# Which of the sums of weights in two gate pairs is made by a transfer and which by VectorE, and the order in which their chunks are loaded

## The chip, the cores and the metric

The kernel runs on one core of one Trainium2 chip. The metric is the device time of one execution in microseconds (us); the time of a kernel is the median of several runs. Beside it stands one execution taken with the hardware profiler, which gives the time of every instruction and transfer.

## The reference

One decoder block on 512 tokens of width 1024, in float32. Its largest part is a projection of the normalised input by one wide weight matrix; two branches use slices of it, and sigmoid gates merge them:

```python
hn = rmsnorm(x, g_mix)
proj = einsum('bsd,de->bse', hn, w_in)          # 1024 x 14344
(xa, ba, ca, za, q, k, v, o, zb, ig, fg, ga, gb) = split(proj)
ya = (ba * causal_short_conv(ca * xa) * silu(za)) @ w_a_out
hb = mlstm_chunkwise(q, k, v, ig + .., fg + ..)  # 4 heads
yb = (sigmoid(o) * rmsnorm(hb) * silu(zb)) @ w_b_out
merged = sigmoid(ga) * ya + sigmoid(gb) * yb
x = x + merged @ w_o
x = x + sigmoid(rmsnorm(x) @ w_ple_gate) * (p @ w_ple)
out = rmsnorm(x)
```

The change concerns the slices for `gb` and `ga`, each 1024 columns wide: the two gate pairs of this document.

## The kernel before

**Split numbers.** Each product in float32 is made of three matmuls of a shorter type (`mm3`, L215). Every operand is therefore cut into a high part, a copy made by ScalarE (ACT, `whi`, L164), and a low part, the rest, made by VectorE (DVE, `wlo`, L165).

**Chunks and operands.** Weights come from HBM in chunks of 512 rows by 512 columns (1 MB, 128 partitions of four row blocks), into four slots of a pool `wraw` (NRAW, L33). The list `chunks` holds the chunks in the order in which they are loaded; the list `operands` holds what TensorE (PE) uses one after the other, each entry with the sums that are to be made after it has been split.

**Pairs.** Two column ranges p1 and p2 form a pair (`pair`, L84). Its weights are a 2 x 2 block matrix: b11 and b21 are the upper and lower 512 rows of p1, b12 and b22 those of p2. `strassen` (L305) multiplies such a pair in seven products (0 to 6) in place of eight, which needs sums of weights. In the kernel before, for a gate pair: product 0 uses b11; then b11 += b12; product 1 uses b21; product 2 uses b11, then b11 += b22; product 3 uses b22, and b12 += b22 is made; product 4 uses b11, then b11 += b21; product 5 uses b12; product 6 uses b11. A sum is made either by DVE (L169, both chunks lie in slots) or by a transfer that reads the chunk from HBM and adds it to what the slot holds, issued from GpSimd's queue (POOL, L171). `on_dve` says which: 0 all by transfers, 1 the third sum (b12 += b22) by DVE, 2 the others too. With 2, which only the two gate pairs have (L108), DVE made b11 += b12, b11 += b22 and b12 += b22, and a transfer made b11 += b21.

**The order of the work.** All engines but the load queue (SP) follow the order in which the program is written. `strassen` issues the matmuls of half a product (one PSUM bank), then calls `step` and through it `tick` (L200): first work on the results of the half before, then one half of the split of the next operand (`split_half`, L162), then the generators in `active`. So operand j + 1 is split while product j runs, one half (256 of its 512 rows) in each tick, and the sums that are listed with an operand follow the split of the same half. The split tiles exist twice (`wsplit`, two buffers).

**Loads.** When the second half of operand i has been split, `done(i)` (L175) gives back the chunks whose last use it was (`last_use`, L129) and `load_free` (L148) loads the next chunks of the list into the free slots, on SP (L144). A chunk that DVE reads as an addend is in use until that sum; one that a transfer adds is read from HBM and needs no slot for it. In the gate pairs before, slots came free after the splits for products 1, 3, 5 and 6.

**Beside the gate pairs.** A gate pair (GB in head 0's turn, GA in head 2's) follows the pair of the ZB columns of two heads, whose last results are still worked on while product 0 and 1 of the gate pair run (`sink_z`, L964: two multiplications by DVE per tile, L968 or L972 and L973, and stores of `z_d` on POOL's queue, L969). In the gate pair itself run: the transposes of the finished head (`turn`, L788, L799), the sigmoid of the gate and its store on ACT's queue (`sink_gate`, L767, L770, L771), and the reload and split of the next head's q and k (`recut`, L808: transfers on SP, L814, after 7 ticks; split by ACT and DVE in four further ticks, L224 and L225). Behind the gate pair comes the pair V and O of the next head, with all sums by transfers.

Of the kernel before, what the change touches and what calls it, by code (L numbers as in the profile page):

```python
# [29 lines left out]
HC = 4  # L30
# [6 lines left out]
def hybrid_block(ctx, tc, x, p, g_mix, w_in, conv_w, conv_b, w_a_out, b_gates, g_head,  # L37
# [31 lines left out]
    chunks, operands = [], []  # L69
    H2 = S // 2  # L70

    def chunk(view, k0, pieces):
        got, pos = [], 0
        for c, n in pieces:
            got.append((view[:, k0:k0 + HC, c:c + n], slice(0, HC), slice(pos, pos + n)))
            pos += n
        chunks.append(got)
        return len(chunks) - 1
# [5 lines left out]
    def pair(view, p1, p2, on_dve=0):  # L84

        where = ((p1, 0), (p2, 0), (p1, HC), (p2, HC)) if on_dve == 2 else ((p1, 0), (p1, HC), (p2, 0), (p2, HC))
        b11, b21, b12, b22 = (chunk(view, k, p) for p, k in where)
        if on_dve == 2:  # L90
            b12, b21 = b21, b12
        e2, e3 = (dve if on_dve >= n else None for n in (2, 1))
        t3 = [(b12, b22, e3)]
        operands.extend([(b11, [(b11, b12, e2)]), (b21, [] if e3 else t3), (b11, [(b11, b22, e2)]),
                         (b22, t3 if e3 else []), (b11, [(b11, b21, None)]), (b12, []), (b11, [])])


    chunks.append([(w_ple_v[:, k:k + 1, n * CW:(n + 1) * CW], slice(2 * n + k, 2 * n + k + 1), slice(0, CW))
# [5 lines left out]
    for h in range(NH):  # L104
        pair(w_in_v, [(V + h * DV, DV)], [(O + h * DV, DV)])
        if h % 2 == 0:
            pair(w_in_v, [(ZB + h * DV, DV)], [(ZB + (h + 1) * DV, DV)])
            pair(w_in_v, [((GB, GA)[h // 2], CW)], [((GB, GA)[h // 2] + CW, CW)], 2)  # L108
        elif h == 1:
            pair(w_in_v, *([(Q + i * DK, DK), (K + i * DK, DK)] for i in (2, 3)), 1)  # L110
    for c in range(0, KT * P, 2 * P):
        pair(w_in_v, *([(o + c, 2 * P) for o in os] for os in ((XA, CA), (BA, ZA))), 1)
    for n in range(2):
        block(w_a_v, [(n * CW, CW)])

    b11, b21, b22, b12 = ([chunk(w_b_v, (2 * g + r) * HC, [(n * CW, CW)]) for g in range(2)]
                          for r, n in ((0, 0), (1, 0), (1, 1), (0, 1)))
# [1208 lines left out]
```

## Time and profile before

| | us |
|---|---|
| median of 3 runs | 864.0 (863.95 to 864.03) |
| the profiled execution: its own time | 863.96 |
| the profiled execution: span from its first to its last instruction | 862.2 |
| mean granted clock of TensorE in it | 0.997 |
| first gate pair and what adjoins it | about 155 to 210 |
| second gate pair and what adjoins it | about 379 to 434 |

Moved bytes: 167.58 MB in 100,138 packets, of them 70.86 MB on POOL's queue (q0) and 90.97 MB on SP's (q1).

How to read the rows below. A row of a timeline has the start in us, the duration in us, the engine, the line, the operation, the output and inputs by the program's names with their shape, and the count; in brackets stands how long the engine was idle before it and what released it. A row of a stretch has from and to, its length, then for each engine its busy time and its number of instructions, and at the end TensorE's granted clock, the busy share of the DMA engines and GB/s. A row of the chain of waits has start, duration and what it was. PE is TensorE (matmuls), PEld its weight loads, DVE VectorE, ACT ScalarE, POOL GpSimd, SPq the load queue. Idle time on an engine that isn't the bottleneck costs nothing.

### The profile page before, as it was taken

The page shows a single profiled execution, that of the slowest core. Times are in us where ns is not written, and L with a number is a line of the kernel's source. Part 1 is how long each engine was busy: PE and PEld are TensorE (multiplying, and loading weights), DVE is VectorE, ACT ScalarE, POOL GpSimd, SP SyncE. Part 2 cuts the span into 40 slices and gives each one's busy share as a digit, 9 for nine tenths or more (in the row PEclk, how much of TensorE's full clock was granted, in tenths as well). Part 3 has the DMA queues.
Part 4 walks back from the last instruction along what each step waited for, and adds up shares of the span by engine and source line. Part 5 has one row for each costly group of instructions (what it writes and reads, how often), then busy time and mean ns, then how long its engine had stood idle before and what let it go on. Part 6 is the DMA issues. An engine that isn't in the chain of part 4 may idle for free.

```text
span 862.2 us, 12152 instructions
## 1 busy us (share of the span) xinstructions
PE 849.0 (98%) x4658; PEld 735.8 (85%) x4658; DVE 630.4 (73%) x813; ACT 483.9 (56%) x702; POOL 218.0 (25%) x221
## 2 busy tenths in 40 slices
PE   9999999999999999999999999999999999999996
PEld 7888888787889988878788999999998888888885
DVE  5786667966767576778568679897986778964465
ACT  7467655657755566565675555545453256634343
POOL 5103222113224322211214323333410212130031
PEclk9999999999999999999999999999999999999998
DMA  9749669589968998775999599899997487884002
GB/s 311 265 135 187 156 133 222 184 235 254 256 135 199 240 224 181 182 183 201 260 243 226 109 243 152 205 175 187 182 346 285 100 196 192 224 319 151 1 1 97
DMA packets 100138, 167.58 MB, mean 194 GB/s; under 512 B 5420, under 2 KB 45920, under 8 KB 98800
## 3 DMA queue, kind: packets, MB, share of 16 engines
q0 software_dynamic: 38672, 70.86, 42.3%
q1 hardware_dynamic: 58544, 90.97, 32.2%
q10 hardware_dynamic: 2864, 4.98, 1.6%
q8 instruction: 36, 0.59, 0.3%
q14 instruction: 22, 0.18, 0.1%
HBM read 150.01 MB, written 16.78 MB: 193 GB/s over the span
## 4 chain that ended last, share of the span: by engine, by line
PE 83%; issue 6%; DVE 4%; DMA 4%; ACT 3%; ACTq 0%; POOL 0%; SPq 0%; POOLq 0%; DVEq 0%
PE mm L218 25%; PE mm L217 25%; PE mm L219 25%; DMA wraw<-in_w_in 2%; DVE wlo L165 1%; PE pv L217 1%; PE pv L218 1%; PE pv L219 1%; ACT whi L164 1%; DMA xin<-in_x 1%; DMA z_d<-c 1%; PE sc L219 1%; PE sc L218 1%; PE sc L217 1%; DVE wraw L169 1%
## 5 line engine op out<-in xcount | busy, mean ns | idle before, releaser
L165 DVE TENSOR_TENSOR wlo<-wraw,whi 128x1024 fp32r<-128x1024 f32 x238 | 298.2, 1256 | 123.0 <-ACT whi L164 121.9
L164 ACT ACTIVATE whi<-wraw 128x1024 fp32r<-128x1024 f32 x240 | 250.8, 1054 | 105.2 <-PE mm L219 45.3
L171 POOL DMA_DIRECT2D wraw<-in_w_in x112 | 136.7, 1416 | 310.0 <-DVE wlo L165 227.1
L333 ACT ACTIVATE s<-mm 128x512 f32<-128x512 f32 x84 | 50.2, 598 | 99.9 <-PE mm L219 97.8
L217 PE MATMUL mm<-whi,hs 128*128 128x512 f32 x256 | 99.9, 390 | 0.0
L218 PE MATMUL mm<-wlo,hs 128*128 128x512 f32 x256 | 99.8, 390 | 0.0
L219 PE MATMUL mm<-whi,hs 128*128 128x512 f32 x256 | 99.7, 389 | 0.0
L217 PE MATMUL mm<-hn_hi,whi 128*128 128x256 f32 (+1 forms) x304 | 93.4, 307 | 0.0
L219 PE MATMUL mm<-hn_hi,wlo 128*128 128x256 f32 (+1 forms) x304 | 93.0, 306 | 0.0
L218 PE MATMUL mm<-hn_lo,whi 128*128 128x256 f32 (+1 forms) x304 | 92.9, 306 | 0.0
L217 PE MATMUL mm<-hs,whi 128*128 128x256 f32 x320 | 90.9, 284 | 0.0
L218 PE MATMUL mm<-hs,whi 128*128 128x256 f32 x320 | 90.5, 283 | 0.0
L219 PE MATMUL mm<-hs,wlo 128*128 128x256 f32 x320 | 90.5, 283 | 0.0
L218 PE MATMUL mm<-wlo,hn_hi 128*128 128x512 f32 x192 | 75.9, 396 | 3.1 <-DVE wlo L165 2.8
L217 PE MATMUL mm<-whi,hn_hi 128*128 128x512 f32 x192 | 75.6, 394 | 0.0
L219 PE MATMUL mm<-whi,hn_lo 128*128 128x512 f32 x192 | 74.9, 390 | 0.0
L218 PEld LDWEIGHTS mm<-hs,whi 128*128 128x128 f32 x320 | 61.4, 192 | 0.0
L217 PEld LDWEIGHTS mm<-hs,whi 128*128 128x128 f32 x320 | 61.4, 192 | 0.0
L219 PEld LDWEIGHTS mm<-hs,wlo 128*128 128x128 f32 x320 | 61.4, 192 | 0.0
L219 PEld LDWEIGHTS mm<-hn_hi,wlo 128*128 128x128 f32 x304 | 58.1, 191 | 2.8 <-POOL wlo L165 0.3
L218 PEld LDWEIGHTS mm<-hn_lo,whi 128*128 128x128 f32 x304 | 58.1, 191 | 2.4
L217 PEld LDWEIGHTS mm<-hn_hi,whi 128*128 128x128 f32 x304 | 58.1, 191 | 2.3
(306 smaller groups left out, 1673.9 us busy)
## 6 DMA issues: line engine op xcount, KB each, us to landing
wraw<-in_w_in SPq DMA_DIRECT2D x32, 1024.0 KB, 5.6
wraw<-in_w_in POOLq DMA_DIRECT2D x52, 512.0 KB, 7.9
wraw<-in_w_in SPq DMA_DIRECT2D x48, 512.0 KB, 5.3
wraw<-in_w_in POOLq DMA_DIRECT2D x60, 256.0 KB, 5.8
wraw<-in_w_b_out SPq DMA_DIRECT2D x7, 1024.0 KB, 6.2
wraw<-in_w_b_out POOLq DMA_DIRECT2D x12, 512.0 KB, 6.6
yt_d<-yc POOLq DMA_DIRECT2D x4, 1024.0 KB, 4.9
wraw<-in_w_a_out SPq DMA_DIRECT2D x4, 1024.0 KB, 6.1
```

The source lines that it names most:

```text
L164: act.activation(hi, t, AF.Copy)
L165: (e_lo or dve).tensor_tensor(lo, t, hi.bitcast(F32), ALU.subtract)
L169: eng.tensor_tensor(raws[to][:, ks, :], raws[to][:, ks, :], raws[c][:, ks, :], ALU.add)
L171: nc.gpsimd.dma_start(raws[to][:, ks, cs], src[:, ks, :], accum_op=ALU.add)
L217: pe.matmul(ps, lhsT=a[0], rhs=b[0], start=first, stop=False, **kw)
L218: pe.matmul(ps, lhsT=a[0], rhs=b[1], start=False, stop=False, **kw)
L219: pe.matmul(ps, lhsT=a[1], rhs=b[0], start=False, stop=last, **kw)
L333: act.activation(to[i], src, AF.Copy, scale=scale)
```

## The change

For `on_dve` 2 the chunks are listed in the order b11, b21, b22, b12 (before: b11, b12, b21, b22). The sum after product 0's operand, b11 += b12, becomes an adding transfer; the sum after product 4's, b11 += b21, becomes an addition by DVE. The second and third sum stay with DVE. Since b21 is now an addend of DVE, its slot is in use until the split for product 4; slots come free after the splits for products 3, 4, 5 and 6. b12 has to lie in its slot by the third sum, at product 3.

```diff
-        where = ((p1, 0), (p2, 0), (p1, HC), (p2, HC)) if on_dve == 2 else ((p1, 0), (p1, HC), (p2, 0), (p2, HC))
+        where = ((p1, 0), (p1, HC), (p2, HC), (p2, 0)) if on_dve == 2 else ((p1, 0), (p1, HC), (p2, 0), (p2, HC))
         b11, b21, b12, b22 = (chunk(view, k, p) for p, k in where)
         if on_dve == 2:
-            b12, b21 = b21, b12
+            b12, b22 = b22, b12
         e2, e3 = (dve if on_dve >= n else None for n in (2, 1))
         t3 = [(b12, b22, e3)]
-        operands.extend([(b11, [(b11, b12, e2)]), (b21, [] if e3 else t3), (b11, [(b11, b22, e2)]),
-                         (b22, t3 if e3 else []), (b11, [(b11, b21, None)]), (b12, []), (b11, [])])
+        operands.extend([(b11, [(b11, b12, None)]), (b21, [] if e3 else t3), (b11, [(b11, b22, e2)]),
+                         (b22, t3 if e3 else []), (b11, [(b11, b21, e2)]), (b12, []), (b11, [])])
```

For the other values of `on_dve` the order and the sums are the same as before.

## The prediction

> **What bounds the kernel now.** I read the page first, then the busy time of three equal stretches: one without a gate pair, and one round each of the two gate pairs that the change touches.
>
> ```profile
> span 862.2 us, 12152 instructions
> PE 849.0 (98%) x4658; PEld 735.8 (85%) x4658; DVE 630.4 (73%) x813; ACT 483.9 (56%) x702; POOL 218.0 (25%) x221
> ...
> 100.00:155.00 55.00, 55.00 (x248) 45.70 (x247) 37.86 (x52) 33.50 (x49) 11.93 (x12) 1.00 0.78 182
> 155.00:210.00 55.00, 53.44 (x238) 42.61 (x237) 41.26 (x44) 35.23 (x49) 9.42 (x10) 1.00 0.76 222
> 379.00:434.00 55.00, 53.46 (x238) 42.56 (x237) 40.73 (x44) 35.27 (x49) 9.35 (x10) 1.00 0.77 223
> 160.00:168.00 8.00, 7.52 (x31) 5.33 (x30) 7.93 (x10) 5.58 (x7) 0.54 (x1) 1.00 0.17 66
> ```
>
> PE is the bound, at full granted clock (1.00), so time can only come from its pauses. Between 100 and 155 us it has none; in both gate stretches it has, and by nearly the same amount (53.44 and 53.46 of 55). The busy column understates the pauses, since a matmul is drawn about 0.4 us long while they start 0.23 us apart; so I read the starts in the first gate pair.
>
> ```profile
> 155.01 0.39 PE L217 MATMUL mm<-whi,hn_hi 128*128 128x512 f32 x1
> ...
> 160.22 0.39 PE L219 MATMUL mm<-whi,hn_lo 128*128 128x512 f32 x1
> 160.45 0.39 PE L217 MATMUL mm<-whi,hn_hi 128*128 128x512 f32 x1
> 161.18 0.50 PE L218 MATMUL mm<-wlo,hn_hi 128*128 128x512 f32 x1 [0.34 <-DVE wlo L165]
> 161.52 0.40 PE L219 MATMUL mm<-whi,hn_lo 128*128 128x512 f32 x1
> ...
> 166.76 0.40 PE L217 MATMUL mm<-whi,hn_hi 128*128 128x512 f32 x1
> 167.29 0.50 PE L218 MATMUL mm<-wlo,hn_hi 128*128 128x512 f32 x1
> ...
> 172.23 1.03 PE L799 MATMUL pty<-ident,gty 128*128 128x128 f32 x8
> 173.02 0.48 PE L217 MATMUL mm<-whi,hs 128*128 128x512 f32 x1
> ...
> 196.39 0.39 PE L217 MATMUL mm<-whi,hn_hi 128*128 128x512 f32 x1
> 197.10 0.50 PE L218 MATMUL mm<-wlo,hn_hi 128*128 128x512 f32 x1 [0.33 <-DVE wlo L165]
> ...
> 202.45 0.39 PE L217 MATMUL mm<-whi,hn_hi 128*128 128x512 f32 x1
> 203.60 0.50 PE L218 MATMUL mm<-wlo,hn_hi 128*128 128x512 f32 x1 [0.76 <-DVE wlo L165]
> ```
>
> Every pause is at a matmul that wants the low half of a weight split (wlo). A regular start follows the last by 0.227 us (23 steps from 155.01 to 160.22, and 160.22 to 160.45 again). Against that, the first pause costs 161.18 - 160.45 - 0.23 = 0.50, and 0.11 more as the pipe refills (161.52 follows by 0.34): 0.61 us. With the same 0.11, the others cost 0.41, 0.59 and 1.03. The four make 2.64 us. By place they are: product 0 (A) and product 1 (B) of the gate pair, product 6 (C), and product 0 of the V/O pair behind it (D). Products of a pair are counted 0 to 6 here, and each weight block is split in two halves.
>
> What released these low halves is shown by the chain of waits in the same stretch:
>
> ```profile
> 155.58 1.23 DVE wlo L165
> 156.83 1.23 DVE wraw L169
> ...
> 159.90 1.23 DVE wlo L165
> 161.16 1.23 DVE wraw L169
> ...
> 181.86 9.80 DMA wraw<-in_w_in
> ...
> 197.73 1.05 ACT whi L164
> ...
> 201.23 1.07 ACT whi L164
> 202.32 1.24 DVE wlo L165
> 203.60 0.50 PE mm L218
> ```
>
> A and B come from DVE, which has no gap there (7.93 of 8.00 us busy from 160 to 168) and has to do the two halves of "b11 += b12" (L169, 156.83 and 161.16) between the splits. C and D come from a transfer: "b11 += b21", issued at 181.86, lands 9.80 us later, and only then can ACT split the sum for product 6:
>
> ```profile
> 163.15 1.05 ACT L164 ACTIVATE whi<-wraw 128x1024 fp32r<-128x1024 f32 x1
> ...
> 165.90 2.00 ACT L164 ACTIVATE whi<-wraw 128x1024 fp32r<-128x1024 f32 x2
> ...
> 191.74 1.06 ACT L164 ACTIVATE whi<-wraw 128x1024 fp32r<-128x1024 f32 x1 [1.51 <-DMA wraw<-in_w_in]
> 192.71 0.61 ACT L224 ACTIVATE qk<-qk_raw 128x512 fp32r<-128x512 f32 x1
> ```
>
> ACT loses 1.51 us at 191.74 and, being full with q/k cuts, sigmoids and its own DMA issues, doesn't make it up before the split at 201.23.
>
> **The change part by part.** Nothing is removed in all: per gate pair two DVE adds of 1.23 us and two 512 KB adding transfers change places, and the chunks are loaded in the order b11, b21, b22, b12.
>
> *The DVE adds leave product 0.* The second low half of product 0 stands behind one of them: from 159.90 it moves to 158.7, and its matmul could start at 161.18 - 1.23 = 159.95, before PE asks for it (160.45 + 0.23 = 160.68). A goes. B's low half stands behind both adds; ACT has its high half at 163.15 + 1.05 = 164.2, so the low half ends at about 165.5, while PE arrives at 166.76 + 0.23 - 0.61 = 166.4. B goes: 0.61 + 0.41 = 1.02 us.
>
> *The DVE adds arrive in product 4's split.* There DVE waits for ACT and PE:
>
> ```profile
> 180.33 2.36 DVE L165 TENSOR_TENSOR wlo<-wraw,whi 128x1024 fp32r<-128x1024 f32 x2 [0.36 <-ACT whi L164]
> 183.93 1.23 DVE L165 TENSOR_TENSOR wlo<-wraw,whi 128x1024 fp32r<-128x1024 f32 x1 [1.23 <-ACT whi L164]
> 187.55 0.69 DVE L337 TENSOR_TENSOR c<-s,mm 128x512 f32<-128x512 f32 x1 [2.39 <-ACT s L333]
> ```
>
> The idle time is 0.36 + 1.23 + 2.39 = 3.98 us, the adds take 2.46: hidden. Product 5's first split would slide from 183.93 to about 185.2, four us before that product starts. Without this cover they would cost what A and B cost now.
>
> *The adding transfer leaves product 4.* The sum is then ready in SBUF by about 185, so ACT's 1.51 us go, and every step of ACT's run behind it is that much earlier. C (0.59) goes. For D the low half's matmul could start at 203.60 - 1.51 = 202.09; PE, itself earlier by C, arrives at 202.45 + 0.23 - 0.59 = 202.09. That is an exact tie, so I leave 0.2 of D's 1.03: 0.59 + 0.83 = 1.42 us.
>
> *The adding transfer arrives in product 0.* POOL issues one half after the low half at 155.58 (so at 156.8), the other after that at 158.7 (so at 159.9). Both must land before ACT splits product 2, now 165.90 and about 166.9, then 0.6 earlier. That leaves 8.5 and 6.4 us. How long such a transfer takes, and what else goes on:
>
> ```profile
> DMA to landing us min/median/max: 4.4/6.2/13.7
> ...
> z_d<-c POOLq DMA_DIRECT2D x3, 256.0 KB, 3.4
> ```
>
> The first row is for all adding transfers of the program (L171). The second is the three POOL stores between 155 and 168, in the middle of DVE's full stretch. In 160 to 168 the DMA engines are busy 0.17, so I take the median or less: no wait. A late landing is also cushioned. Product 2 starts at 173.02 and wants its second low half 7 matmuls on, at 174.6, less the 1.0 gained: 173.6. From ACT's split to that matmul takes 203.60 - 201.23 = 2.37, so the sum may land at 171.2, 11.3 us after its issue. On POOL the new issues precede the z_d stores of the pair before, which wait for later DVE work anyway; nothing queued there is held.
>
> *The loads.* A slot now comes free at products 3, 4, 5, 6 instead of 1, 3, 5, 6 (b21 is kept for the late add). The next pair's first chunk takes the place that its second has now, on SP:
>
> ```profile
> 179.25 0.34 SPq L814 DMA_DIRECT2D qk_raw<-qk_d  x1
> 180.05 0.37 SPq L144 DMA_DIRECT2D wraw<-in_w_in  x1
> ...
> DMA to landing us min/median/max: 3.3/7.8/10.5
> ```
>
> It is wanted at 197.73, less the gain: 16 us after 180, enough. The second chunk waits for the moved add (about 185) and is wanted a product later than the first. Within the gate pair each chunk is loaded at least as early, relative to its first use, as now. The q/k reloads (L814; their time to landing is the last row) stay where they are if SP keeps its order. No cost.
>
> *Sum.* Per pair 1.02 + 1.42 = 2.44. The count of matmuls allows a check: 238 instructions in 55 us, 16 of them short transposes (eight take 0.79 us, from 172.23 to 173.02), 222 x 0.227 + 1.6 = 52.0, so about 3.0 are lost where I can name 2.64. Of the other 0.4 (small hesitations at product starts, some of them at the transposes, which stay) I take 0.3. The two gate pairs are alike (53.44 and 53.46), so 2 x 2.74 = 5.5 us. The profiled execution took 863.96 (its span of 862.2 and 1.8 round it, which the change doesn't touch), the median is 864.0: **858.5 us**.
>
> **The rivals.** *Half the gain.* If SP's new order puts the second chunk's load ahead of the q/k reloads, these are issued after the moved add, at about 185 instead of 179 on, and land 7.8 later, at about 193, where ACT wants them at 192.71 - 1.51 = 191.2, and earlier still by the 1.0 gained. One DMA wait of ACT replaces the other, and C and D stay: 863.96 - 2 x 1.02 = 861.9, or 861 with part of the small ones. For it: in program order the freed slot's load does come just before the reloads. Against: SP's present order has the first reload ahead of a load that was due two steps before it. Chance 0.11.
>
> *No change.* The pauses at A and B go, but PE then only reaches a later limit sooner: ACT's run from 191.74 to 201.23 has no slack, so if it is bound by something else than the 1.51, C and D grow by what A and B gave back. 864 within 0.2%. Against: ACT was idle for 1.51 us right before that run, so it starts it without arrears. This case also covers the case that the order of the queues leaves the adds where they cost the same. Chance 0.08.
>
> *Slower: the moved transfer lands late.* Place: ACT's split for product 2. Each us past 11.3 costs 2 (two pairs); past 14.0 the gain is used up, past 14.9 the kernel is slower by over 0.2%. The largest landing of any adding transfer is 13.7. [...] Against: the three z_d stores in the same full stretch, issued by the same queue, landed in 3.4 us. [...] Chance 0.05.
>
> **How the numbers follow.** The forecast has the remaining 0.76. Its own range is 857.4 (all of the 3.0 and a little more per pair) to 860.0 (D and the small ones stay). To hold 8 in 10 the range reaches to the half gain: 857.3 to 862.0. A change under 0.2% (1.7 us) can't be told from none here, so faster means below 862.3: the forecast and nearly all of the half gain, 0.86; same 0.08; slower 0.06, the late landing and a little for what isn't thought of.
>
> **What would show it.** Right: matmul starts at A, B and C 0.23 us apart; PE about 54.5 or more of 55 busy in both gate stretches; DVE adds at about 181 and 184, none at 156 to 162; two POOL transfers at about 157 and 160 landing in under 7 us; ACT's split for product 6 without a DMA wait. Wrong: ACT waiting for a DMA at product 2's split or at the q/k cuts, PE pauses of new origin at products 2 or 3, or the pauses C and D as long as now.

## The result and the profile after

The changed kernel takes 858.0 us (857.67 to 858.62, 6 runs), the kernel before 864.31 us in the same comparison (863.95 to 865.08, 6 runs). The ratio is 0.9926, with a 95% interval of 0.9914 to 0.9939: about 6.3 us less, where the prediction had said 858.5 us. The profiled execution spans 856.3 us (before 862.2).

The stretches that hold the gate pairs, and the eight us in which DVE had been full, in the kernel after (columns as before; 376 to 431 is the second gate pair, which now starts 3 us earlier):

```profile
155.00:210.00 55.00, 55.00 (x250) 45.05 (x249) 42.58 (x45) 35.55 (x50) 10.82 (x11) 1.00 0.82 231
...
376.00:431.00 55.00, 55.00 (x250) 45.06 (x249) 42.57 (x45) 35.59 (x50) 10.85 (x11) 1.00 0.83 232
160.00:168.00 8.00, 8.00 (x39) 6.66 (x38) 7.08 (x10) 4.14 (x6) 1.78 (x2) 1.00 0.92 191
```

PE no longer pauses visibly (55.00 of 55, before 53.44 and 53.46) and gets 250 instructions into the stretch where 238 fitted. DVE has gaps from 160 to 168 (7.08 of 8, before 7.93). The DMA engines, which had been busy 0.17 there, are busy 0.92: POOL's queue alone, with the moved transfer and the `z_d` stores. At the places of A and B the matmuls follow without a pause, as these steps of the kernel after show:

```profile
160.66 0.39 PE L217 MATMUL mm<-whi,hn_hi 128*128 128x512 f32 x1
160.88 0.39 PE L218 MATMUL mm<-wlo,hn_hi 128*128 128x512 f32 x1
...
166.10 0.39 PE L217 MATMUL mm<-whi,hn_hi 128*128 128x512 f32 x1
166.32 0.39 PE L218 MATMUL mm<-wlo,hn_hi 128*128 128x512 f32 x1
```

DVE, POOL, ACT and SP in the first gate pair after, for the steps that the prediction named:

```profile
158.84 1.22 DVE L165 TENSOR_TENSOR wlo<-wraw,whi 128x1024 fp32r<-128x1024 f32 x1
...
180.46 1.23 DVE L169 TENSOR_TENSOR wraw<-wraw,wraw 128x1024 f32<-128x1024 f32 x1
...
182.85 1.23 DVE L169 TENSOR_TENSOR wraw<-wraw,wraw 128x1024 f32<-128x1024 f32 x1
```
```profile
157.30 1.23 POOL L171 DMA_DIRECT2D wraw<-in_w_in  x1 [1.62 <-DVE wlo L165]
...
160.36 1.19 POOL L171 DMA_DIRECT2D wraw<-in_w_in  x1 [1.24 <-DVE wlo L165]
```
```profile
165.43 1.05 ACT L164 ACTIVATE whi<-wraw 128x1024 fp32r<-128x1024 f32 x1
168.10 1.06 ACT L164 ACTIVATE whi<-wraw 128x1024 fp32r<-128x1024 f32 x1 [1.61 <-DMA wraw<-in_w_in]
...
188.50 0.60 ACT L333 ACTIVATE s<-mm 128x512 f32<-128x512 f32 x1 [1.17 <-PE mm L219]
188.99 1.05 ACT L164 ACTIVATE whi<-wraw 128x1024 fp32r<-128x1024 f32 x1
```
```profile
178.20 0.34 SPq L814 DMA_DIRECT2D qk_raw<-qk_d  x1
178.91 0.37 SPq L144 DMA_DIRECT2D wraw<-in_w_in  x1
```

The low half that waited at 159.90 is made at 158.84, the adds run at 180.46 and 182.85, and the split for product 6 (188.99) follows the PSUM copy without a DMA wait. SP kept its order. One thing is new: ACT now waits 1.61 us for a transfer at the split for product 2 (168.10).

A ruler for the rest of this text is the matmul that opens the scores of a head (`pnb`, L835): its four starts in the trace cut the program into the two gate stretches, the stretch between them and the tail. The columns are in us; all rows come from one profiled execution each, and the last column is the median of all executions.

| kernel | 1st gate stretch | between | 2nd gate stretch | last `pnb` to last matmul | median, us |
|---|---|---|---|---|---|
| before | 131.51 | 92.41 | 131.57 | 419.33 | 864.31 |
| after | 128.52 | 92.41 | 128.51 | 419.33 | 858.0 |
| both by transfer | 131.45 | 92.48 | 130.01 | 419.31 | 862.1 |
| both by DVE | 129.97 | 93.10 | 129.89 | 419.31 | 860.9 |
| new sums, old order | 128.52 | 93.01 | 128.51 | 419.31 | 858.47 |
| old sums, new order | 135.56 | 92.63 | 134.88 | 419.34 | 871.81 |
| first transfer late | 132.38 | 92.45 | 130.91 | 420.05 | 865.18 |
| first transfer a plain copy | 128.52 | 92.41 | 128.53 | 419.30 | 858.04 |
| before, gate stores on POOL | 131.30 | 94.16 | 131.42 | 419.57 | 865.49 |
| after, gate stores on POOL | 128.32 | 92.43 | 128.30 | 420.79 | 858.96 |
| before, gate stores on SP | 129.94 | 93.86 | 130.13 | 420.05 | 863.15 |
| after, gate stores on SP | 128.31 | 92.41 | 128.30 | 419.34 | 857.59 |

All of the gain lies in the two gate stretches, 2.99 and 3.06 us; the stretch between and the tail have the same length to 0.01 us, and what precedes the first `pnb` is 0.2 us longer in the trace of the kernel after (79.12 beside 78.91).

A gate stretch can be cut once more, at the first transposes of the finished head (L799, at 168.58 in the kernel before): A and B lie ahead of them, C and D behind.

| kernel | 1st and 2nd gate stretch, up to the transposes (A, B) | from the transposes on (C, D) |
|---|---|---|
| before | 89.67 and 89.63 | 41.84 and 41.94 |
| after | 88.34 and 88.35 | 40.18 and 40.16 |
| both by transfer | 88.34 and 88.35 | 43.11 and 41.66 |
| both by DVE | 89.76 and 89.69 | 40.21 and 40.20 |
| before, gate stores on SP | 89.70 and 89.63 | 40.24 and 40.50 |

So A and B with the small pauses near them were worth 1.3 us in each stretch, C and D 1.7 to 1.8.

### The profile page after: what moved, and what is told of

It reads as the page before. It is cut to its first block, busy times and chain, and to the rows that moved or that the text cites. A ratio compares the mean times of both kernels' runs of the same rounds, so it can differ in the third digit from the quotient of the medians.

```text
span 856.3 us, 12144 instructions
## 1 busy us (share of the span) xinstructions
PE 845.6 (99%) x4658; PEld 735.4 (86%) x4658; DVE 630.3 (74%) x813; ACT 483.4 (56%) x702; POOL 218.1 (25%) x221
## 4 chain that ended last, share of the span: by engine, by line
PE 95%; DVE 2%; DMA 1%; issue 1%; ACT 1%; SPq 0%; POOL 0%; POOLq 0%; ACTq 0%
PE mm L217 29%; PE mm L218 29%; PE mm L219 29%; PE pv L217 1%; PE pv L219 1%; PE pv L218 1%; DMA xin<-in_x 1%; PE pty L799 1%; PE sc L219 1%; PE sc L218 1%; PE sc L217 1%; PE ptk L1135 0%; PE pth L1102 0%; PE pt L536 0%; DVE xin L531 0%
## 5 line engine op out<-in xcount | busy, mean ns | idle before, releaser
L333 ACT ACTIVATE s<-mm 128x512 f32<-128x512 f32 x84 | 50.2, 598 | 100.9 <-PE mm L219 99.6
```

The costliest lines, as they stand in the source:

```text
L333: act.activation(to[i], src, AF.Copy, scale=scale)
```

## The experiments

The theory: DVE's two adds in product 0 made pauses A and B, the late transfer of product 4 made C and D, and the order of the chunks alone brings nothing. Rival 1: the gain comes from the other order of loads and slots. Rival 2: ACT is full from product 5 on, whatever the transfer does. The kernel before took 864.19 to 864.42 us in the comparisons below.

### One half of the change at a time

Both sums by transfers, order of the chunks as in the changed kernel (the passages of code from here on are shortened):

```diff
-  (b22, t3 if e3 else []), (b11, [(b11, b21, e2)]), ...      # changed kernel
+  (b22, t3 if e3 else []), (b11, [(b11, b21, None)]), ...
```

> First and last sum of the gate pairs both by adding transfers, chunks in the new order. My theory (DVE's adds in product 0 made pauses A and B, the late transfer of product 4 made C and D, the order of the chunks alone brings nothing): A and B go, C and D stay, so about 862.0 us (861.3 to 862.7) against 864.3 before. Rival 1 (the gain comes from the new order of loads and slots): this kernel has the new order, so 858 to 859. Rival 2 (ACT is full from product 5 on, whatever the transfer does): 862 as well.

Measured: 862.1 us, ratio 0.9974 (0.9965 to 0.9984). Pauses A and B are gone in both gate stretches (88.34 and 88.35 up to the transposes); C and D stand. ACT, then PE, around C in the first gate stretch of this kernel:

```profile
191.67 1.06 ACT L164 ACTIVATE whi<-wraw 128x1024 fp32r<-128x1024 f32 x1 [2.53 <-DMA wraw<-in_w_in]
```
```profile
194.83 0.50 PE L217 MATMUL mm<-whi,hn_hi 128*128 128x512 f32 x1 [0.88 <-ACT s L333]
...
196.32 0.40 PE L217 MATMUL mm<-whi,hn_hi 128*128 128x512 f32 x1
197.28 0.50 PE L218 MATMUL mm<-wlo,hn_hi 128*128 128x512 f32 x1 [0.56 <-DVE wlo L165]
```

The pause C is 0.96 - 0.227 = 0.73 here, more than before (0.48 without the refill), and a larger one stands ahead of it: at 194.83, 1.28 us after the matmul before it, PE waits for a PSUM bank that ACT has still to copy (L333), and that copy stands in ACT's queue behind the split that waited 2.53 us for the transfer, instead of 1.51. So the first gate stretch gives the gain of A and B back from the transposes on (43.11 beside 41.84), through a later landing. In the second (131.57 to 130.01, 1.56 us) it is kept, with 0.28 more behind the transposes that is not A and B. The new order of loads is in this kernel, and 862.1 is not 858: rival 1 is out as the whole cause.

Both sums by DVE, order of the chunks as before:

```diff
-  (b22, t3 if e3 else []), (b11, [(b11, b21, None)]), ...    # kernel before
+  (b22, t3 if e3 else []), (b11, [(b11, b21, e2)]), ...
```

> First and last sum of the gate pairs both by DVE, chunks in the old order. My theory: A and B stay, C and D go: about 861.2 us (860.5 to 862.0); with the kernel that has both by transfer the two gains add up to that of the whole change (6.3 us). Rival 1 (order of loads): old order, so 864. Rival 2 (ACT full anyway): C and D stay, 864, or above it by what the two added DVE sums cost.

Measured: 860.9 us, ratio 0.9960 (0.9949 to 0.9972). A and B stand, with C gone and only the same rest of D as in the changed kernel (40.21 and 40.20 from the transposes on). A in this kernel:

```profile
160.38 0.39 PE L217 MATMUL mm<-whi,hn_hi 128*128 128x512 f32 x1
161.20 0.50 PE L218 MATMUL mm<-wlo,hn_hi 128*128 128x512 f32 x1 [0.43 <-DVE wlo L165]
```

C and D go once the transfer is gone, so rival 2 falls too: beyond the rest of D, ACT makes no pause there without the late transfer. What ACT adds to it is shown further down. The ratios multiply to 0.9974 x 0.9960 = 0.9934, beside 0.9926 for the whole change: within their intervals the two halves add up.

### The order of the chunks alone

New sums in the old order:

```diff
-  where = ((p1, 0), (p1, HC), (p2, HC), (p2, 0)) if on_dve == 2 else ...   # changed kernel
+  where = ((p1, 0), (p2, 0), (p1, HC), (p2, HC)) if on_dve == 2 else ...
-      b12, b22 = b22, b12
+      b12, b21 = b21, b12
```

> The sums of the changed kernel with the chunks in the old order b11, b12, b21, b22. My theory: 858.0 us within 0.5, since each chunk still lands well before its first use. Rival 1: most of the gain goes, 862 to 864.

Measured: 858.47 us, ratio 0.9932 (0.9919 to 0.9945), not to be told from the changed kernel. The gate stretches are the same to 0.01 us (the stretch between is 0.6 us longer in this trace, by a pause in the V/O pair). So the order isn't needed for the gain in the gate pairs; up to half a us elsewhere these runs leave open.

Old sums in the new order, the reverse edit on the kernel before:

> The sums of the kernel before with the chunks in the new order b11, b21, b22, b12. My theory: no gain, and a loss: DVE's first add needs b12, which is now the fourth chunk, issued at 154.0 and landing about 5 us later, at 159, where DVE wants it at 156.8. DVE and the split behind it come 2.3 us later in each pair, pause A grows by that: about 869 us (866 to 871). Rival 1 (the order brings the gain): below 863.

Measured: 871.81 us, ratio 1.0090 (1.0074 to 1.0105). The direction is as expected, the size just outside the stated 866 to 871. DVE's wait is 2.69 us where 2.3 were expected, and PE's pause follows from it; here the DVE rows and the PE rows of the first gate pair, and the ten us around:

```profile
155.72 1.22 DVE L165 TENSOR_TENSOR wlo<-wraw,whi 128x1024 fp32r<-128x1024 f32 x1
159.63 1.23 DVE L169 TENSOR_TENSOR wraw<-wraw,wraw 128x1024 f32<-128x1024 f32 x1 [2.69 <-DMA wraw<-in_w_in]
```
```profile
163.97 0.50 PE L218 MATMUL mm<-wlo,hn_hi 128*128 128x512 f32 x1 [3.00 <-DVE wlo L165]
164.31 0.46 PE L219 MATMUL mm<-whi,hn_lo 128*128 128x512 f32 x1
164.57 0.63 PE L217 MATMUL mm<-whi,hn_hi 128*128 128x512 f32 x1
164.99 0.63 PE L218 MATMUL mm<-wlo,hn_hi 128*128 128x512 f32 x1
165.42 0.63 PE L219 MATMUL mm<-whi,hn_lo 128*128 128x512 f32 x1
```
```profile
160.00:170.00 10.00, 7.00 (x25) 5.29 (x24) 9.90 (x13) 3.98 (x6) 1.08 (x2) 0.83 0.14 52
```

The wait of 2.69 us explains some 5 of the 7.6 us lost. The rest is a thing that the expectation didn't have: behind the pause the matmuls start 0.43 us apart instead of 0.227, for about 3 us, and the granted clock is 0.83 over these ten us. The load order thus matters only with the old sums, as the first of them reads b12 from its slot.

### How late the moved transfer may land

The adding transfer of product 0 is held until product 1's low half exists; a small POOL operation that reads it stands in front:

```diff
-  (b11, [(b11, b12, None)]), (b21, [] if e3 else t3), ...
+  (b11, [] if e2 else [(b11, b12, None)]), (b21, [(b11, b12, "late")] if e2 else [] if e3 else t3), ...
+  # in split_half, for "late": active.append(late_add(to, c, h, lo))
+  def late_add(to, c, h, lo):
+      pool.tensor_tensor(scr, lo[:, 0, :4].bitcast(F32), mhalf, ALU.mult)
+      nc.gpsimd.dma_start(raws[to][:, ks, cs], src[:, ks, :], accum_op=ALU.add)
```

> The changed kernel, but the adding transfer of product 0 in the gate pairs is issued only after the low half of product 1's split is made (a small POOL operation that reads it stands in front), about 6 us later (164 to 166 instead of 157 and 160). My theory (ACT's wait at product 2's split, 1.6 us in the changed kernel, is cushioned until about 171.3): landing at about 173.7, 2.4 us late, in two pairs: 862.8 us (860 to 866). Rival (no cushion, each us that ACT waits is a us of PE): 5.7 later twice, 869.

Measured: 865.18 us, ratio to before 1.0008 (0.9997 to 1.0020): 7.2 us more than the changed kernel, so the whole gain is used up. That lies in the wide range given with the theory (860 to 866) but 2.4 us above its figure, and below the rival's 869; the rows show why neither has the mechanism. ACT, DVE and PE in the first gate pair (this kernel's L349 is L337 of the others):

```profile
169.69 1.06 ACT L164 ACTIVATE whi<-wraw 128x1024 fp32r<-128x1024 f32 x1 [4.19 <-DMA wraw<-in_w_in]
172.56 1.06 ACT L164 ACTIVATE whi<-wraw 128x1024 fp32r<-128x1024 f32 x1 [1.82 <-DMA wraw<-in_w_in]
```
```profile
170.78 1.23 DVE L165 TENSOR_TENSOR wlo<-wraw,whi 128x1024 fp32r<-128x1024 f32 x1 [5.13 <-ACT whi L164]
172.04 1.22 DVE L172 TENSOR_TENSOR wraw<-wraw,wraw 128x1024 f32<-128x1024 f32 x1
173.18 0.68 DVE L349 TENSOR_TENSOR c<-s,mm 128x512 f32<-128x512 f32 x1
```
```profile
171.03 1.03 PE L811 MATMUL pty<-ident,gty 128*128 128x128 f32 x8
174.01 0.47 PE L228 MATMUL mm<-whi,hs 128*128 128x512 f32 x1 [1.94 <-DVE c L349]
...
176.32 0.63 PE L230 MATMUL mm<-whi,hs 128*128 128x512 f32 x1
176.75 0.63 PE L228 MATMUL mm<-whi,hs 128*128 128x512 f32 x1
```

There is a cushion, but it ends sooner, and elsewhere than I had it. What PE waits for is not the split but a PSUM bank: product 2 writes into the bank of product 1, which DVE empties at 173.18. In DVE's queue that read stands behind the low half of the *first* half of product 2 and the add after it, and these wait for ACT, which waits for the transfer. It is the same kind of wait as at 194.83 in the kernel with both sums by transfers. Besides, in this first gate pair the pause was followed by matmuls 0.43 us apart again; the second gate stretch, without that, lost 2.40 us against 3.86 in the first.

### What the adding costs the transfer

The transfer of product 0 copies b12 over b11 in place of adding it, so products 2, 4 and 6 of the gate pairs work on other weights:

```diff
-  nc.gpsimd.dma_start(raws[to][:, ks, cs], src[:, ks, :], accum_op=ALU.add)
+  nc.gpsimd.dma_start(raws[to][:, ks, cs], src[:, ks, :])
```

> The changed kernel, but the transfer of product 0 in the gate pairs copies b12 over b11 in place of adding it (so products 2, 4 and 6 work on other weights). It measures what the adding costs a transfer of 512 KB. My theory: landing drops from 7.6 to below 5 us, ACT's wait of 1.6 us at product 2's split goes, and the time stays at 858.0 within 0.5 since that wait is cushioned. Rival (ACT's wait costs PE time): 2 x 1.6 us less, 855.

Measured: 858.04 us, ratio 0.9924 (0.9911 to 0.9936), the same as the changed kernel. The median times to landing between 155 and 168 us, with the adding transfer (kernel after) and with the copy:

```profile
wraw<-in_w_in POOLq DMA_DIRECT2D x2, 512.0 KB, 7.6
```
```profile
wraw<-in_w_in POOLq DMA_DIRECT2D x2, 512.0 KB, 5.7
```

The kernel with the copy in the eight us from 160, columns as in the rows of the result:

```profile
160.00:168.00 8.00, 8.00 (x41) 6.74 (x40) 7.09 (x9) 4.99 (x7) 1.17 (x2) 1.00 0.55 166
```

And ACT's row for the split of product 2 in the same kernel, both halves in one row:

```profile
164.96 2.00 ACT L164 ACTIVATE whi<-wraw 128x1024 fp32r<-128x1024 f32 x2
```

The copy lands 1.9 us sooner, if not below 5 us as was expected, and occupies the DMA engines for 0.55 of those eight us instead of 0.92. ACT's wait of 1.61 us at the split for product 2 is gone, both halves run back to back at 164.96, and the time hasn't moved: that wait in the changed kernel costs nothing.

### What holds D: ACT's own issues

The gate stores (`sg_d`, L771) moved from ACT's queue, first to POOL's, in the kernel before and in the changed one:

```diff
-  nc.scalar.dma_start(sg_d[g + n][:, t, :], sg)
+  nc.gpsimd.dma_start(sg_d[g + n][:, t, :], sg)
```

> The kernel before, with the stores of the gates (sg_d) issued from POOL's queue in place of ACT's. ACT saves about 0.7 us in each tick that has such a store. My theory: ACT's wait for the transfer (1.5 us) and pause C stay as they are, D shrinks since ACT makes up its arrears in the two ticks from C to D: 864.3 - 2 x (0.8 to 1.0) = 862.5 us (862 to 863.3). Rival 2 (ACT is full from product 5 on, the transfer doesn't matter): C goes too, 861 or below. If DVE or DMA hold D instead of ACT: 864.3.

Measured: 865.49 us, ratio 1.0013 (1.0003 to 1.0023): not faster. D did go in this trace, but the first gate stretch is only 0.21 us shorter. ACT waits for the second half of the late transfer as well, C grows by what D gave, and two pauses come in the V/O pair behind, the larger of them shown here; ACT, then PE:

```profile
195.50 1.06 ACT L164 ACTIVATE whi<-wraw 128x1024 fp32r<-128x1024 f32 x1 [1.07 <-DMA wraw<-in_w_in]
```
```profile
197.87 0.50 PE L218 MATMUL mm<-wlo,hn_hi 128*128 128x512 f32 x1 [0.77 <-DVE wlo L165]
...
236.63 0.50 PE L218 MATMUL mm<-wlo,hs 128*128 128x512 f32 x1 [0.52 <-DVE wlo L165]
```

> The changed kernel with the stores of the gates issued from POOL's queue. My theory: only the rest of D (0.2 us per pair) can go: 857.6 us, hardly to be told from 858.0. Any larger change would show that ACT's run still bounds the second half of the gate pairs.

Measured: 858.96 us, ratio 0.9934 (0.9921 to 0.9948). The gate stretches are 0.2 us shorter each, as expected, but the tail is 1.46 us longer, again from pauses in a V/O pair. So the moved stores cost elsewhere. To see whether POOL's queue was the reason, the same stores on SP's queue:

> The kernel before, with the gates' stores issued from SP's queue (the load queue) in place of ACT's. In the run with these stores on POOL's queue pause D went, but C grew by as much and new pauses came in the V/O pair, both at splits that waited for an adding transfer. If that came from sharing POOL's queue with the adding transfers, then here D goes without that: 864.3 - 2 x (0.8 to 1.0) = 862.5 us (861.8 to 863.2). If it came from ACT running ahead and then waiting for the same transfers, it comes here too: 864 to 865.5. C (0.59 and the hesitation before it) stays in both cases, since the transfer of product 4 lands no earlier.

Measured: 863.15 us, ratio 0.9981 (0.9972 to 0.9990), at the edge of what was expected. D is gone, and most of C too, which the expectation had left whole: gate stretches 129.94 and 130.13, and 40.24 and 40.50 from the transposes on, where both by DVE has 40.21 and 40.20. So nearly as much is won behind the transposes with the late transfer still in place (ACT still waits 1.35 us for its first half, but not for its second, as it did with the stores on POOL): C and D take both, the late landing and ACT's own issues behind it. The pauses in the V/O pairs came here as well (93.86 in place of 92.41, and 420.05).

> The changed kernel with the gates' stores issued from SP's queue. Only the rest of D (0.2 us per pair) can go: 857.6 us if sharing POOL's queue was what cost 1 us in the run with the stores on POOL, 858.5 to 859 if it was ACT running ahead, more if loads queued behind the stores come late.

Measured: 857.59 us (857.50 to 857.89), ratio 0.9919 (0.9906 to 0.9933). The gate stretches have their shortest length, 128.31 and 128.30, and no V/O pause is in the trace. It has the lowest median here, but by 0.4 us, which these intervals can't tell from the changed kernel.

The V/O pauses stay open. Some of them stand right behind a split that waited for one of the V/O pair's own adding transfers (1.65 us in the kernel before with stores on POOL, ahead of the first pause); but in the changed kernel ACT waits 1.66 us at that split, and no pause follows. Two kernels with none of the stores moved have such a pause too: new sums in the old order (93.01 between the gate stretches) and both by DVE (93.10, there behind a reload of `z_d` for which DVE waited 2.06 us). Neither queue nor ACT's lead alone goes with them.

## Why the prediction was right, point by point

- *A and B from DVE's adds.* Right: gone when the adds move (both by transfer, 1.33 and 1.28 us up to the transposes). The term was 1.02 plus a share of the small hesitations; it had left out a small third pause behind the same adds, at product 1's first low half (165.50 follows by 0.30 in the kernel before).
- *C and D from the late transfer.* Right: both by DVE removes them, 1.63 and 1.74 us from the transposes on, beside 1.42 plus a share of the small ones. The part that the prediction gave to ACT's full run holds as well: with the gate stores on SP's queue most of C and all of D go although ACT still waits for the transfer.
- *0.2 of D stays.* So it came, but by luck in the size: the working gave an exact tie, and 0.2 was a guess. With the gate stores off ACT's queue this rest goes too. D in the kernel after, 0.30 + 0.34 - 2 x 0.227 = 0.19 us:

```profile
200.54 0.39 PE L217 MATMUL mm<-whi,hn_hi 128*128 128x512 f32 x1
200.84 0.50 PE L218 MATMUL mm<-wlo,hn_hi 128*128 128x512 f32 x1
201.18 0.40 PE L219 MATMUL mm<-whi,hn_lo 128*128 128x512 f32 x1
```

- *The adds are hidden in product 4.* Right: 180.46 and 182.85, no pause of PE behind them.
- *The loads cost nothing.* Right in the gate pairs: with the new sums, both orders of the chunks give the same gate stretches.
- *No wait at product 2's split, landing at the median or less.* Wrong, and the prediction itself had named this wait as a sign of being wrong. The two halves landed 7.6 and 7.7 us after their issue and ACT waited 1.61 us. The median of 6.2 was taken over adding transfers of all sizes; the page of the kernel before has those of the gate pairs' size apart, and by that row 7.6 is nothing unusual:

```profile
wraw<-in_w_in POOLq DMA_DIRECT2D x52, 512.0 KB, 7.9
...
wraw<-in_w_in POOLq DMA_DIRECT2D x60, 256.0 KB, 5.8
```

The step also took the low DMA share (0.17) as room, but the transfer itself raised it to 0.92. The cushion hid the wait, as the plain copy shows: the mechanism of the gain stood, one step on the way to it did not.
- *Nothing queued on POOL is held.* Wrong, at no cost: the `z_d` stores between 155 and 168 us landed in 7.5 us (median) behind the adding transfers, where they had taken 3.4; with the plain copy 5.7.
- *The cushion of 11.3 us.* Wrong in kind. It was worked out from the second half's split; the limit that came first is the PSUM bank of product 1, behind two DVE operations that wait for the first half. The cushion is smaller than 11.3 us; by how much, these runs do not give. In the first gate pair the slow matmuls behind the pause raised the price past it as well (3.86 us lost beside 2.40).
- *The sum.* 2 x 2.74 = 5.5 predicted, 2.99 and 3.06 in the trace. Both pairs of pauses were named too small (1.02 for 1.3, 1.42 for 1.7 to 1.8), and the 0.3 allowed for small hesitations covers half of that.
- *The slower rival.* Not seen: POOL issued the two transfers in 1.23 and 1.19 us at 157.30 and 160.36, while DVE worked without a gap (155.17 to 165.68), they landed 7.6 and 7.7 us after their issue where the rival put a slower kernel past 14.9, and the DMA engines were 0.92 busy from 160 to 168.

## What to carry to other kernels

Where the bound engine shows a few short pauses, read which queue released each one: a sum of the same work can sit on a full engine in one step (DVE at product 0, 7.93 of 8 us busy) and on an idle one a few steps later (DVE at product 4, idle for 3.98 us), and here moving it cost nothing, since both its inputs and the transfers had room there. A busy share measured without a transfer said little about how long the transfer would take there (0.17 without it, 0.92 with it, 7.6 us to landing), and a median over transfers of several sizes said little about one size (6.2 us over all, 7.9 at 512 KB). The slack of a wait was set by everything that stood behind it in each engine's queue, PSUM banks to be emptied included (with the first transfer late, PE sat idle for 1.94 us until DVE had emptied one), not by the one consumer that one has in mind.

## What the runs showed of the hardware

- A pause of about 3 us of PE was followed by about 3 us of matmuls at about half the rate (0.43 us apart in place of 0.227, from 393.35 to 396.34 in the second gate pair; granted clock 0.83 over ten us in the first), in both gate pairs of the kernel with old sums in new order (idle 3.00 and 3.09 us, the matmuls on both sides starting 3.39 and 3.48 us apart). In the kernel with the late transfer, 3.21 us from the last full matmul to the next, transposes between them, had this effect in the first gate pair (granted clock 0.79 from 172 to 180), and 3.13 us in the second did not (1.00 from 394 to 403). The pauses of about a us in the kernel before did not have it (1.00 in both gate stretches). Why one of two waits of nearly the same length had it and the other not, these runs do not show.
- An adding transfer of 512 KB took 7.6 us to land where a plain copy from the same queue at the same place took 5.7, and the DMA engines were busy 0.92 of the eight us from 160 against 0.55, with the `z_d` stores in both.
